# Gated recurrence of the second block: one half of the tokens reversed, both halves in one matmul per level

## The chip, the cores and the metric

The kernel runs on one core of a Trainium2 chip. Its time is the device time of one execution, in microseconds; of several runs the median is taken. Before the change it is 829.94 us (three runs, 829.58 to 829.96).

## What is computed

The reference is a chain of blocks on 256 tokens of width 1024, all in fp32: a block with a linear recurrence and a feed-forward part, a block with stick-breaking attention and a feed-forward part, and then a "second block" with two branches side by side, a block attention (moba) and a gated linear recurrence (hgrn). The change is in the last of these. Cut to what matters:

```python
kb = (1.0 - lb) * jax.nn.sigmoid(-fpre)            # 4 heads, 128 key dims
qb = jax.nn.silu(bq)                               # queries
vb = bi                                            # values
# per chunk of 64 tokens, g = log_f, the logarithm of the forget gate
cum = jnp.cumsum(gc, axis=2)
o_inter = jnp.einsum('bhtk,bhkv->bhtv', qc * jnp.exp(cum), state)
diff = jnp.where(causal[:, :, None], cum[:, :, :, None, :] - cum[:, :, None, :, :], LOG_DECAY_MASK)
scores = jnp.einsum('bhtk,bhsk,bhtsk->bhts', qc, kc, jnp.exp(diff))
o_intra = jnp.einsum('bhts,bhsv->bhtv', scores, vc)
last = cum[:, :, -1:, :]
state = state * jnp.exp(last[:, :, 0, :, None]) + jnp.einsum('bhsk,bhsv->bhkv', kc * jnp.exp(last - cum), vc)
```

So the score of query t and key s is a sum over 128 dimensions of q times k times the product of the forget gates between s and t.

## The kernel before, in words

**Matmuls.** Every large product is done as three fp32r matmuls: weights and activations are split into a high part and a remainder (wh and wl, xh and xl), and high x high, low x high and high x low are added in PSUM. Weights come in 266 pieces of 512 KB, loaded by SP's queue some pieces ahead (`load_ahead`). ACT or DVE rounds them to wh (`round`), and DVE subtracts to get wl (`tt` at L239). All matmuls but the transposes are recorded by the helper `mm` at L281 to L283, so they share one line of the profile and are told apart by their tiles.

**Order.** The program is written by a planner (`Run`). The matmul stream is the main thread. Work of other engines stands in small tasks (`spawn`) that yield the planner's time at which they may go on; between two products the planner polls them (`poll`, L343) and then rounds weights ahead (`prep_ahead`, L461). Its clocks for PE, DVE and ACT come from costs that are written in the code. What it leaves is a fixed queue for each engine, and each queue runs in order.

**The second block.** `proj4` (L1278) projects four groups of 128 columns into PSUM and `evac` (L1270) multiplies with the row of norm factors on DVE: queries `qb`, forget gates `fb`, and further on `aq`, `ag`, `bg`, `ak` for the attention and the output gates. `proj_t` (L1295) does the same with tokens on the partitions, for values (`vbt`); its evacuation on ACT scales with a column. `ORDER_E` (L50) sets the order of these groups after queries and gates: aq, g0, bi, ag, bg, ak, g1, g2, g3, av, ple. In the matmul stream they alternate with the recurrence, which is spread among them by the planner.

**The recurrence** works by levels instead of chunks. `diag` (L1359) multiplies keys and queries of each of the four heads and each half of 128 tokens (eight 128 x 128 products) and keeps the diagonal in `dg`. Then, for a level of block size b = 1, 2, 4, ... 64 and at last 128, a key of an earlier block meets a query of the later block next to it. `levels` (L1415) keeps keys K (tile ga_) and queries Q (tile hq) in place: after each level it multiplies the keys of earlier blocks and the queries of later blocks by the gate products of a block (tiles gf_ and ht). `level_scores` (L1376) does a level's matmuls: for b under 32 (LONE) one for each head and each half, all 128 keys against the 64 queries in later blocks:

```python
for g in range(8 if b < LONE else 0):
    a, i = divmod(g, 2)
    rhs = Q[:, a, 128 * i:128 * i + 128].rearrange("p (n two b) -> p n two b", two=2, b=b)[:, :, 1, :]
    r.mm(bank.t[:, 64 * g:64 * g + 64], K[:, a, 128 * i:128 * i + 128], rhs, bank.start(), True)
```

A masked copy on DVE (L1408) then puts the blocks that belong together into `dg`. For b of 32 and 64 each pair of blocks has its own matmul, and ACT copies the result. Level 128 takes the keys of the first half to the queries of the second, and ACT copies it to `xg`. `hgrn_out` (L1580) multiplies values with `dg` and `xg`, twelve matmuls. An fp32 matmul (not fp32r) shows in the trace as two records. In between stand the small groups of the attention's head norms: `hsq` with a constant (sums of squares), and `rtx` with `sel` (roots spread over the rows).

Of the kernel before, what the change touches and what calls it, by code (L numbers as in the profile page):

```python
# [107 lines left out]
LEVELS = [1, 2, 4, 8, 16, 32, 64]  # L108

# [7 lines left out]
def make_consts():  # L117
# [13 lines left out]
    m = np.zeros((128, 7 * 64), np.int32)  # L131
    for n, b in enumerate(LEVELS):
        t = np.array([t for t in range(128) if t % (2 * b) >= b])
        m[:, n * 64:(n + 1) * 64] = (p[:, None] // (2 * b) == t[None, :] // (2 * b)) & (p[:, None] % (2 * b) < b)
# [53 lines left out]
class Run:  # L188
# [324 lines left out]
    def gemm_t(self, banks, name, k, ms, x, stop):  # L513

        self.need(x, f"{name} {k}")
        wh, wl = self.weight(name, k, ms)
        for t, b in enumerate(banks):
            s = slice(128 * t, 128 * t + 128)
            self.mm(b.t, x.hi[:, s], wh, b.start(), False)
            self.mm(b.t, x.lo[:, s], wh, False, False)  # L520
            self.mm(b.t, x.hi[:, s], wl, False, stop)
            self.tick()
# [33 lines left out]
def build(r):  # L556
# [9 lines left out]
    msk = r.one("msk", [128, 448], I32)  # L566
# [703 lines left out]
    def evac(bank, dst, done=None, more=None):  # L1270
        yield r.pe_t + 0.2
        yield norm.s
        t = r.tt(dst, v2(bank), bc2(norm.S), OP.mult)
        r.free(bank, t)
        if done is not None:
            done.t = t

    def proj4(base, dst, done, outer=False, tag="acc"):  # L1278

        if outer:  # L1280
# [4 lines left out]
            for p in range(2):  # L1285
                r.spawn(evac(bs[p], dst[:, 2 * p:2 * p + 2], done[p]))
        else:
            for p in range(2):
# [4 lines left out]
                r.spawn(evac(b, dst[:, 2 * p:2 * p + 2], done[p]))  # L1293

    def proj_t(base, vs):  # L1295
# [4 lines left out]
        for k in range(8):  # L1300
            r.gemm_t(bs, "w_in2", k, quad(base), norm.x[k], k == 7)

        def chain(t):
            yield r.pe_t + 0.2
            yield norm.s
            f = r.act(vs[t].v, bs[t].t, AF.Copy, scale=norm.col[:, t:t + 1])
# [6 lines left out]
    qb, fb = r.big("qb"), r.big("fb")  # L1313
    q_done, f_done, aq_done, ak_done, ag_done, bg_done = ([Fut(), Fut()] for _ in range(6))
    vbt, va = [Fut(), Fut()], [Fut(), Fut()]
    proj4(16, qb, q_done, True, "g")
# [17 lines left out]
    proj4(20, fb, f_done)  # L1334

    def forget():
        yield f_done

        A, N, F = r.big("ga_"), r.big("gn_"), r.big("gf_")
# [5 lines left out]
        for c in range(4):  # L1345
            t = r.ts(A[:, c], A[:, c], oml[:, c:c + 1], None, OP.mult)
# [3 lines left out]
        for c in range(4):  # L1350
            r.ts(N[:, c], N[:, c], lbv[:, c:c + 1], 1.0, OP.mult, OP.add)
# [4 lines left out]
    dg, xg = r.big("dg", [128, 8, 128]), r.big("xg", [128, 4, 128])  # L1356
    dgf, lvl = Fut(), [Fut() for _ in range(8)]

    def diag():  # L1359
        yield [qf, kf, Avail("g", 2)]  # L1360
        for i in range(2):
            b = r.bank("g")
            for g in range(4):
                c = slice(128 * (g % 2), 128 * (g % 2) + 128)
                a = 2 * i + g // 2
                r.mm(b.t[:, 128 * g:128 * g + 128], hg["K"][:, a, c], qb[:, a, c], b.start(), True)
            yield r.pe_t + 0.2
            t = r.tt(dg[:, 4 * i:4 * i + 4], b.t.rearrange("p (a b) -> p a b", b=128),
# [4 lines left out]
    def halves(ap, b):  # L1373
        return ap.rearrange("p h (n two b) -> p (h n) two b", two=2, b=b)

    def level_scores(n, b, K, Q):  # L1376
        yield Avail("g", 1)
        bank = r.bank("g")
        if b == 128:
            for a in range(4):  # L1380
                r.mm(bank.t[:, 128 * a:128 * a + 128], K[:, a, 0:128], Q[:, a, 128:256], bank.start(), True)
# [5 lines left out]
        for g in range(8 if b >= LONE else 0):  # L1387
            a, i = divmod(g, 2)
            for j in range(64 // b):
                o = 128 * i + 2 * b * j  # L1390
                r.mm(bank.t[2 * b * j:2 * b * j + b, 64 * g + b * j:64 * g + b * j + b], K[:, a, o:o + b],
                     Q[:, a, o + b:o + 2 * b], g == 0, True)
        for g in range(8 if b < LONE else 0):
            a, i = divmod(g, 2)
            rhs = Q[:, a, 128 * i:128 * i + 128].rearrange("p (n two b) -> p n two b", two=2, b=b)[:, :, 1, :]
# [414 lines left out]
```

## Time and profile before

| | |
|---|---|
| median of three runs | 829.94 us |
| profiled execution, its own time | 829.69 us |
| its span, from the first to the last instruction | 828.0 us |
| granted TensorE clock, mean | 0.999 |
| TensorE matmuls busy | 821.9 us (99%) |
| weight loads busy (beside matmuls) | 734.5 us (89%) |
| VectorE busy | 627.6 us (76%) |
| ScalarE busy | 388.1 us (47%) |
| GpSimd busy | 23.9 us (3%) |
| chain of work that ended last: TensorE's share | 96% |

The span is cut into windows where single stretches are read; the recurrence lies between 617 and 662 us of it, among the projections of the second block. A row of the time line names start, length, engine, line, operation and tiles; a matmul's length includes the depth of its pipeline, so the cost of a group is read from its start to the start of the next.

### The profile page before, as it was taken

To read this page: it belongs to the slowest core of one execution; us is meant where nothing else is said; L and a number is where in the kernel's file an instruction comes from. 1 tells how busy PE (TensorE), PEld (TensorE's weight loads), DVE (VectorE), ACT (ScalarE), POOL (GpSimd) and SP (SyncE) were. 2 spreads that over 40 slices of the span, in tenths; PEclk is the share of its full clock that TensorE was granted. 3 is DMA by queue.
4 is the path that set the end of the run, shared out by engine and by line. 5 is a ranking of instruction groups with operands and counts; after the bars stand their busy time and mean duration, and the time that the engine had idled before them with its cause. 6 is when DMAs were issued, how large, how long until landed. Compare 5 with 4: busy or idle time off the path is not lost.

```text
span 828.0 us, 13459 instructions
## 1 busy us (share of the span) xinstructions
PE 821.9 (99%) x5206; PEld 734.5 (89%) x5206; DVE 627.6 (76%) x1213; ACT 388.1 (47%) x735; POOL 23.9 (3%) x56
## 2 busy tenths in 40 slices
PE   9999999999999999999999999999999999999997
PEld 8999988888888898999888888888999999999997
DVE  5999998685764668898899667546788886896872
ACT  4788475241222545565566123115353354686421
POOL 1300000000000001011000000001000000000000
PEclk9999999999999999999999999999999999999999
DMA  8945666654644223355776464543433434456401
GB/s 323 393 145 206 237 221 220 213 206 164 216 149 157 77 102 141 140 179 178 233 251 227 168 215 159 197 152 130 138 123 108 178 129 138 171 201 202 155 2 51
DMA packets 41360, 144.79 MB, mean 175 GB/s; under 512 B 4616, under 2 KB 5904, under 8 KB 41296
## 3 DMA queue, kind: packets, MB, share of 16 engines
q1 hardware_dynamic: 40896, 142.61, 49.1%
q0 software_dynamic: 400, 1.32, 0.5%
q8 instruction: 41, 0.67, 0.3%
q14 instruction: 23, 0.19, 0.1%
HBM read 142.85 MB, written 1.06 MB: 174 GB/s over the span
## 4 chain that ended last, share of the span: by engine, by line
PE 96%; DVE 2%; DMA 1%; ACT 1%; SPq 1%; issue 0%
PE acc L283 51%; PE g L283 42%; PE g L1044 1%; DMA raw<-in_weights 1%; PE g L1199 1%; DVE rec L243 1%; DVE wl L239 0%; PE g L1100 0%; ACT wh L264 0%; PE g L1540 0%; SPq L406 0%; SPq L399 0%; DVE z L239 0%; ACT sq L266 0%; DVE o L239 0%
## 5 line engine op out<-in xcount | busy, mean ns | idle before, releaser
L239 DVE TENSOR_TENSOR wl<-raw,wh 128x512 fp32r<-128x512 f32 x518 | 336.4, 690 | 20.2 <-ACT wh L264 11.5
L264 ACT ACTIVATE wh<-raw 128x512 fp32r<-128x512 f32 x357 | 196.7, 624 | 35.3 <-PE acc L283 18.1
L283 PE MATMUL g<-wh,xh 128*128 128x512 f32 x368 | 144.6, 393 | 0.0
L283 PE MATMUL g<-wl,xh 128*128 128x512 f32 x368 | 143.4, 390 | 0.0
L283 PE MATMUL g<-wh,xl 128*128 128x512 f32 x368 | 143.2, 389 | 0.0
L283 PE MATMUL acc<-xh,wh 128*128 128x256 f32 x416 | 120.5, 290 | 0.0
L283 PE MATMUL acc<-xl,wh 128*128 128x256 f32 x416 | 117.6, 283 | 0.0
L283 PE MATMUL acc<-xh,wl 128*128 128x256 f32 x416 | 117.6, 283 | 0.0
L283 PE MATMUL acc<-wh,hx 128*128 128x512 f32 x352 | 108.8, 390 | 0.0
L283 PEld LDWEIGHTS acc<-xh,wh 128*128 128x128 f32 x416 | 79.5, 191 | 4.4 <-issue 3.9
L283 PEld LDWEIGHTS g<-wl,xh 128*128 128x128 f32 x368 | 69.1, 188 | 14.6
L283 PEld LDWEIGHTS g<-wh,xl 128*128 128x128 f32 x368 | 69.2, 188 | 13.8
L283 PEld LDWEIGHTS g<-wh,xh 128*128 128x128 f32 x368 | 69.1, 188 | 13.8
L283 PEld LDWEIGHTS acc<-xl,wh 128*128 128x128 f32 x416 | 79.7, 192 | 0.1
L264 ACT ACTIVATE hx<-g 128x512 fp32r<-128x512 f32 x22 | 12.1, 596 | 144.4 <-PE g L1044 144.4
L283 PEld LDWEIGHTS acc<-xh,wl 128*128 128x128 f32 x416 | 79.6, 191 | 0.0
L283 PEld LDWEIGHTS acc<-wh,hx 128*128 128x128 f32 x352 | 65.8, 188 | 13.4
L283 PE MATMUL acc<-wl,hx 128*128 128x512 f32 x176 | 68.5, 389 | 0.0
L254 DVE CAST wh<-raw 128x512 fp32r<-128x512 f32 x161 | 68.4, 425 | 0.0
L243 DVE SCALAR_TENSOR_TENSOR gu<-g,ny,gu 128x512 f32<-128x512 f32 (+1 forms) x24 | 16.2, 706 | 54.3 <-PE g L283 54.2
L283 PE MATMUL g<-xh,wh 128*128 128x256 f32 x136 | 39.5, 290 | 0.0
L283 PEld LDWEIGHTS acc<-wl,hx 128*128 128x128 f32 x176 | 33.0, 188 | 6.9
(294 smaller groups left out, 1370.4 us busy)
## 6 DMA issues: line engine op xcount, KB each, us to landing
raw<-in_weights SPq DMA_DIRECT2D x264, 512.0 KB, 3.7
toep<-vrev POOLq DMA_DIRECT2D x2, 512.0 KB, 4.8
raw<-in_weights SPq DMA_DIRECT2D x3, 256.0 KB, 5.0
gh<-in_x SPq DMA_DIRECT2D x3, 256.0 KB, 5.4
past<-in_past SPq DMA_DIRECT2D x1, 384.0 KB, 4.1
raw<-in_weights SPq DMA_DIRECT2D x2, 128.0 KB, 2.4
pt<-in_p POOLq DMA_DIRECT2D x1, 256.0 KB, 5.4
out_y<-o__1285_8421 SPq DMA_DIRECT2D x1, 256.0 KB, 2.4
```

The lines of the kernel that those rows point to most:

```text
L239: self.nc.vector.tensor_tensor(out, a, b, op)
L243: self.nc.vector.scalar_tensor_tensor(out, a, s, b, op0=op0, op1=op1)
L254: self.nc.vector.tensor_copy(out, a)
L264: self.nc.scalar.activation(out, a, f, scale=scale, **kw)
L283: self.nc.tensor.matmul(out, l, r, start=start, stop=stop, skip_group_check=True)
L1044: nc.tensor.transpose(b.t[:, at:at + 128], w[:, t, 256 * p + 128 * i:256 * p + 128 * i + 128], r.ident)
L1199: nc.tensor.transpose(tb[a].t[:, b], m[:, a, b], r.ident)
```

## The change

The second half of the tokens is kept in reverse order throughout the recurrence, and tiles are laid out by half first (`by_half`: 128 partitions, half, head, 128 tokens). In the reversed half the earlier blocks of a level stand where the later ones stand in the first half. So the keys of both halves' earlier blocks together fill 128 columns, and one matmul takes them against the later blocks of both halves. Of its 128 x 128 results the masked copies keep the two parts that belong together. In detail:

- `evac` with `turn` writes `qb` and `fb` in two instructions, the second half reversed. `forget`, `diag` and the products of the levels work on the new layout, with as many instructions as before.
- `stand`: for b = 1, 2, 4, 8, 16 and 64 ACT copies the keys of the earlier blocks of both halves into one operand (tile hm). Then four matmuls, one for each head, replace eight. Level 32 keeps its sixteen small ones, level 128 its four.
- The masked copy on DVE, and the copies on ACT for b of 32 and 64, are done once for each half; the mask grows from 448 to 640 columns (five levels of 128).
- Values must be reversed in their tokens too. `turn_x` copies the second half of the norm's output in reverse (tiles xrh, xrl, four ACT copies), `gemm_t` takes these as the operand of the second token half of `bi`, and `turn_col` reverses the scale row on ACT (tile nr), turns it into a column by a matmul of one column with a constant, and copies it (tile nc).
- `hgrn_out` reads `xg` and the second half of `dg` backwards.

```diff
-    def gemm_t(self, banks, name, k, ms, x, stop):
+    def gemm_t(self, banks, name, k, ms, x, stop, turned=None):
...
+            hi, lo = x.hi[:, s], x.lo[:, s]
+            if turned is not None and t == 1:
+                self.need(turned, "turned")
+                hi, lo = turned.hi, turned.lo
...
-    def evac(bank, dst, done=None, more=None):
+    def evac(bank, dst, done=None, turn=False):
...
+        if turn:
+            r.tt(dst[:, 0], v2(bank)[:, :, 0:128], bc2(norm.S)[:, :, 0:128], OP.mult)
+            t = r.tt(dst[:, 1], v2(bank)[:, :, 128:256][:, :, ::-1], bc2(norm.S)[:, :, 128:256][:, :, ::-1],
+                     OP.mult)
+        else:
+            t = r.tt(dst, v2(bank), bc2(norm.S), OP.mult)
...
+    def turn_col():
+
+        yield norm.s
+        yield Avail("g", 1)
+        row = r.small("nr", 128)
+        yield r.act(row[0:1], norm.S[0:1, 128:256][:, ::-1], AF.Copy) + 0.06
+        b = r.bank("g")
+        r.mm(b.t[:, 0:1], row[0:1], ones128[0:1, 0:1], True, True)
+        yield r.pe_t + 0.2
+        colr.v = r.small("nc", 1)
+        t = r.act(colr.v, b.t[:, 0:1], AF.Copy)
...
+    def turn_x():
+
+        hi, lo = r.big("xrh", [128, 8, 128], F32R), r.big("xrl", [128, 8, 128], F32R)
+        for q in range(2):
+            yield [norm.x[4 * q + i] for i in range(4)]
+            yield r.pe_t + 3.0
+            c = slice(4 * q, 4 * q + 4)
+            for d, s in ((hi, norm.hi[q]), (lo, norm.lo[q])):
+                t = r.act(d[:, c], s[:, :, 128:256][:, :, ::-1].bitcast(F32), AF.Copy)
+                yield t
...
+    def blocks(ap, b, at, step):
+
+
+        (ps, pn), (hs, _), (_, a), (_, n) = ap.ap
+        return bass.AP(tensor=ap.tensor, offset=ap.offset + at, ap=[[ps, pn], [hs + step, 2], [2 * b, a * n // (2 * b)],
+                                                                    [1, b]])
...
+    def stand(n, b, K):
+
+        M[n].v = r.big("hm", [128, 4, 128])
+        src = earlier(K, b).rearrange("p i n b -> p n i b")
+        M[n].t = r.act(M[n].v.rearrange("p a (n i b) -> p (a n) i b", i=2, b=b), src, AF.Copy)
+
     def level_scores(n, b, K, Q):
+        if b < 128 and b != LONE:
+            stand(n, b, K)
+            yield M[n].t + 0.06
...
-        for g in range(8 if b < LONE else 0):
-            a, i = divmod(g, 2)
-            rhs = Q[:, a, 128 * i:128 * i + 128].rearrange("p (n two b) -> p n two b", two=2, b=b)[:, :, 1, :]
-            r.mm(bank.t[:, 64 * g:64 * g + 64], K[:, a, 128 * i:128 * i + 128], rhs, bank.start(), True)
+        nb = 64 // b
+        to = bank.t.rearrange("p (i a t) -> p i a t", i=2, a=4)
...
+        else:
+            for a in range(4):
+                r.mm(to[:, :, a], M[n].v[:, a], later(Q[:, :, a:a + 1], b), bank.start(), True)
...
-            nc.vector.copy_predicated(out, m, src)
-            t = r._v((512 + 66) / 0.96)
+            for i in range(2):
+                m = msk[:, 128 * n + 64 * i:128 * n + 64 * i + 64].rearrange("p (n b) -> p n b", b=b)
+                out = dg[:, i].rearrange("p a (n two b) -> p a n two b", two=2, b=b)[:, :, :, 1 - i]
+                nc.vector.copy_predicated(out, m[:, None].to_broadcast([128, 4, nb, b]),
+                                          to[:, i].rearrange("p a (n b) -> p a n b", b=b))
...
-            k, q = halves(K, b)[:, :, 0, :], halves(Q, b)[:, :, 1, :]
-            r.tt(k, k, Tv[:, :, 1:2].to_broadcast([128, nb, b]), OP.mult)
-            t = r.tt(q, q, Tv[:, :, 0:1].to_broadcast([128, nb, b]), OP.mult)
+            k, q = earlier(K, b), later(Q, b)
+            r.tt(k, k, decays(U, b, 1, -1), OP.mult)
+            t = r.tt(q, q, decays(U, b, 0, 1), OP.mult)
...
-            r.mm(o[:, 128:256], vbt[0].v[:, v], xg[:, a], False, False)
-            r.mm(o[:, 128:256], vbt[1].v[:, v], dg[:, 2 * a + 1], False, True)
+            r.mm(o[:, 128:256], vbt[0].v[:, v], xg[:, a, ::-1], False, False)
+            r.mm(o[:, 128:256], vbt[1].v[:, v], dg[:, 1, a, ::-1], False, True)
...
-            proj_t(24, vbt)
+            proj_t(24, vbt, True)
```

The planner orders the queues anew. The scale's matmul (cst with ny, four) stands six matmuls earlier in PE's queue than before; 21 matmuls of the stream further on stands the new one of one column. Counted from a common point of the stream (70 steps ahead of the scale's matmul before, 64 after), 223 steps of the stream stand ahead of level 1 before and 202 after. The queues are shown at two places. The first is PE at the level with b = 4, which is the third, in the middle of the values' projection (`bi`). There rtx with sel is the first spread of roots, the rows with ga_ or hm are the level, and xrh and xrl are the turned x. Before:

```order
L283 MATMUL acc_6281<-wh_6219,xh_5428 128x512
L283 MATMUL acc_6281<-wh_6219,xl_5430 128x512
L283 MATMUL acc_6281<-wl_6220,xh_5428 128x512
L283 MATMUL g_6299<-hq_6129,ga__952_6001 128x64 x8
L283 MATMUL g_6308<-rtx_6260,sel_5917 128x256 x4
L283 MATMUL acc_6282<-wh_6219,xh_5428 128x512
L283 MATMUL acc_6282<-wh_6219,xl_5430 128x512
```

After:

```order
L288 MATMUL acc_6294<-wh_6273,xh_5428 128x512
L288 MATMUL acc_6294<-wh_6273,xl_5430 128x512
L288 MATMUL acc_6294<-wl_6274,xh_5428 128x512
L288 MATMUL g_6325<-rtx_6292,sel_5928 128x256 x4
L288 MATMUL g_6330<-hq_6118,hm_6313 128x2x64 x4
L288 MATMUL acc_6295<-wh_6273,xrh_5622 128x512
L288 MATMUL acc_6295<-wh_6273,xrl_5623 128x512
```

The spread now stands ahead of the level instead of behind it, the level has four matmuls instead of eight, and six more wide steps of `bi` stand ahead of both.

The second place is ACT from the sums of squares (hsq) to the roots rtx, through the first three levels. Before, no level has a row on ACT here:

```order
L266 ACTIVATE hsq_6152<-aq_5922 128x1024
L264 ACTIVATE wh_6157<-raw_5957 128x512
L277 ACT_TABLE_LOAD
L266 ACTIVATE rt_6180<-g_6170,der 128x256 x2
L266 ACTIVATE rt_6180<-rt_6180 128x256 x2
L264 ACTIVATE wh_6219<-raw_6013 128x512 x2
L264 ACTIVATE rtx_6260<-y_6179 128x256
```

After:

```order
L269 ACTIVATE hm_6168<-ga__955_5998 128x512
L271 ACTIVATE hsq_6178<-aq_5933 128x1024
L269 ACTIVATE wh_6180<-raw_5990 128x512
L282 ACT_TABLE_LOAD
L271 ACTIVATE rt_6217<-g_6203,der 128x256 x2
L271 ACTIVATE rt_6217<-rt_6217 128x256 x2
L269 ACTIVATE hm_6232<-ga__955_5998 128x512
L269 ACTIVATE wh_6234<-raw_6030 128x512
L269 ACTIVATE wh_6273<-raw_6068 128x512
L269 ACTIVATE rtx_6292<-y_6216 128x256
L269 ACTIVATE wh_6273<-raw_6068 128x512
L269 ACTIVATE hm_6313<-ga__955_5998 128x512
```

Three copies of key blocks stand between the rest. On DVE, between the evacuation of `qb` and rtx, there are one rounding and one 128 x 512 instruction more than before; up to hq there are two 128 x 512 instructions less.

## Rows read from the trace of the kernel before

**Rows 1.** The page, busy time of each engine: us, share of the span, instructions.

```profile
PE 821.9 (99%) x5206; PEld 734.5 (89%) x5206; DVE 627.6 (76%) x1213; ACT 388.1 (47%) x735; POOL 23.9 (3%) x56
```

**Rows 2.** Waits of PE in the whole run: us in total, times, longest us.

```profile
PE g L588 <- DVE der L607: 1.1, 1, 1.1
PE acc L283 <- DVE rec L243: 0.4, 1, 0.4
```

**Rows 3.** Windows over the recurrence: us, then busy us (instructions) of PE, PEld, DVE, ACT, POOL; clock, DMA.

```profile
600.00:620.00 20.00, 20.00 (x171) 20.00 (x171) 17.64 (x38) 10.04 (x12) 0.00 (x0) 1.00 0.32 110
620.00:640.00 20.00, 20.00 (x156) 18.67 (x155) 17.91 (x31) 8.88 (x17) 0.00 (x0) 1.00 0.36 129
640.00:660.00 20.00, 20.00 (x177) 18.30 (x176) 17.65 (x33) 5.79 (x11) 0.00 (x0) 1.00 0.49 175
```

**Rows 4.** Time line, PE at levels 1, 64 and 128: start us, length us, instruction, records.

```profile
625.31 1.90 PE L283 MATMUL g<-hq,ga__952_6001 128*128 128x64 f32 x16
627.01 0.36 PE L283 MATMUL acc<-xh,wh 128*128 128x256 f32 x1
...
653.54 1.15 PE L283 MATMUL g<-hq,ga__952_6001 128*64 128x64 f32 x16
654.62 0.39 PE L283 MATMUL acc<-xh,wh 128*128 128x256 f32 x1
...
656.88 1.06 PE L283 MATMUL g<-hq,ga__952_6001 128*128 128x128 f32 x8
657.69 0.36 PE L283 MATMUL acc<-xh,wh 128*128 128x256 f32 x1
```

**Rows 5.** Time line, PE at the norm's sums, four matmuls of one column.

```profile
591.38 0.28 PE L283 MATMUL acc<-xh,wl 128*128 128x256 f32 x1
591.50 0.95 PE L283 MATMUL g<-ones,ssq 128*128 128x1 f32 x8
592.31 0.36 PE L283 MATMUL acc<-xh,wh 128*128 128x256 f32 x1
```

**Rows 6.** Time line, ACT at the last norm and at level 128; in brackets idle before.

```profile
582.64 0.91 ACT L264 ACTIVATE xh<-gh,der 128x256 fp32r<-128x256 f32 x2 [4.12 <-DVE gh L239]
...
657.97 0.60 ACT L264 ACTIVATE xg<-g 128x512 f32<-128x512 f32 x1 [2.13 <-PE g L283]
```

**Rows 7.** Time line, DVE from the evacuation of qb to rtx.

```profile
605.26 1.29 DVE L239 TENSOR_TENSOR qb<-g,S 128x512 f32<-128x512 f32 x2 [2.12 <-ACT S L264]
...
607.66 0.42 DVE L254 CAST wh<-raw 128x512 fp32r<-128x512 f32 x1
608.11 0.69 DVE L239 TENSOR_TENSOR wl<-raw,wh 128x512 fp32r<-128x512 f32 x1
608.72 0.69 DVE L248 TENSOR_SCALAR gn__953_6002<-fb 128x1024 f32<-128x1024 f32 x1
...
621.02 1.22 DVE L239 TENSOR_TENSOR hq<-qb,gf__954_6003 128x1024 f32<-128x1024 f32 x1
...
627.24 0.69 DVE L239 TENSOR_TENSOR ga__952_6001<-ga__952_6001,gf__954_6003 128x512 f32<-128x512 f32 x1 [1.53 <-PE g L283]
...
628.46 0.42 DVE L239 TENSOR_TENSOR ht<-ht 128x256 f32<-128x256 f32 x1
628.79 0.42 DVE L239 TENSOR_TENSOR rt<-rt 128x256 f32<-128x256 f32 x1
...
635.05 0.46 DVE L239 TENSOR_TENSOR rtx<-y,rtx 128x256 fp32r<-128x256 f32 x1
```

**Rows 8.** Instructions on tile dg, the masked copies: duration ns min/median/max, first and last start.

```profile
L1408 DVE COPY_PREDICATED dg<-msk,g x5: 708/720/1322, 629.6 to 648.5; 128x512 f32<-128x512 int32 x5
```

**Rows 9.** Time line, PE in the values' projection and at the first spread.

```profile
633.42 0.40 PE L283 MATMUL acc<-wh,xl 128*128 128x512 f32 x1
633.66 0.39 PE L283 MATMUL acc<-wl,xh 128*128 128x512 f32 x1
...
636.96 0.72 PE L283 MATMUL g<-rtx,sel 128*128 128x256 f32 x4
```

More of the change, by code (lines that the diff above doesn't have):

```diff
@@ L1276, in evac, with proj4 @@
             done.t = t
-    def proj4(base, dst, done, outer=False, tag="acc"):
+    def proj4(base, dst, done, outer=False, tag="acc", turn=False):
         if outer:
@@ L1285, in proj4 @@
             for p in range(2):
-                r.spawn(evac(bs[p], dst[:, 2 * p:2 * p + 2], done[p]))
+                r.spawn(evac(bs[p], two(dst, p, turn), done[p], turn))
         else:
@@ L1292, in proj4, with proj_t @@
                         r.gemm(b, c, "w_in2", k, base + 2 * p + c, norm.x[k], k == 7)
-                r.spawn(evac(b, dst[:, 2 * p:2 * p + 2], done[p]))
-    def proj_t(base, vs):
+                r.spawn(evac(b, two(dst, p, turn), done[p], turn))
+    def proj_t(base, vs, turn=False):
         bs = [r.bank("acc"), r.bank("acc")]
@@ L1300, in proj_t @@
         for k in range(8):
-            r.gemm_t(bs, "w_in2", k, quad(base), norm.x[k], k == 7)
+            r.gemm_t(bs, "w_in2", k, quad(base), norm.x[k], k == 7, turned[k] if turn else None)
         def chain(t):
@@ L1305, in chain @@
             yield norm.s
-            f = r.act(vs[t].v, bs[t].t, AF.Copy, scale=norm.col[:, t:t + 1])
+            col = norm.col[:, t:t + 1]
+            if turn and t == 1:
+                yield colr
+                col = colr.v
+            f = r.act(vs[t].v, bs[t].t, AF.Copy, scale=col)
             r.free(bs[t], f)
@@ L1311, in proj_t, with two @@
             r.spawn(chain(t))
-    qb, fb = r.big("qb"), r.big("fb")
+    def turn_col():
[8 more added lines that the diff above has]
+        t = r.act(colr.v, b.t[:, 0:1], AF.Copy)
+        r.free(b, t)
+        colr.t = t
+    def turn_x():
[7 more added lines that the diff above has]
+                yield t
+            for k in range(4 * q, 4 * q + 4):
+                turned[k].hi, turned[k].lo, turned[k].t = hi[:, k], lo[:, k], t
+    def two(dst, p, turn):
+        return dst[:, :, 2 * p:2 * p + 2] if turn else dst[:, 2 * p:2 * p + 2]
+    colr, turned = Fut(), [Fut() for _ in range(8)]
+    r.spawn(turn_x())
+    r.spawn(turn_col())
+    by_half = [128, 2, 4, 128]
+    qb, fb = r.big("qb", by_half), r.big("fb", by_half)
     q_done, f_done, aq_done, ak_done, ag_done, bg_done = ([Fut(), Fut()] for _ in range(6))
     vbt, va = [Fut(), Fut()], [Fut(), Fut()]
-    proj4(16, qb, q_done, True, "g")
+    proj4(16, qb, q_done, True, "g", True)
     def x2_chain():
@@ L1410, in level_scores @@
         r.free(bank, t)
         lvl[n].t = t
+    M = [Fut() for _ in range(8)]
     read = [Fut() for _ in range(8)]
```

90 lines of the change are left out of this document (48 added, 42 removed).

## The prediction

> **What bounds the kernel now.** I read the page's busy times first, then TensorE's waits, then the time line of the recurrence. TensorE (PE) is busy 99% of the span, VectorE (DVE) comes next with 76% [rows 1]. A modelled busy share proves little by itself, so the list of waits counts more: in the whole run PE waits for another engine twice, 1.1 us at the start and 0.4 us once later [rows 2]. The three windows over the recurrence say the same: PE 20.00 us of 20.00, granted clock 1.00 (the 2.4 GHz level) [rows 3]. So a microsecond taken out of PE's queue here comes out of the time, as long as no other engine comes late. DVE could: it is busy 17.64, 17.91 and 17.65 us in the three windows [rows 3], 53.2 of 60, which leaves 6.8 us. ScalarE (ACT) has 24.7 of 60 and is not short of time.
>
> **The levels on PE.** I name a level by its block size b. Before, a level with b from 1 to 16 is eight matmuls with 128 weight columns and 64 moving columns: 16 records, from 625.31 to the next group at 627.01, 1.70 us, 106 ns a record [rows 4]; the other four levels have the same row. After, such a level is four matmuls with 128 weight columns and 128 moving columns. That shape is in the trace: level 128 has four of them, 8 records, from 656.88 to 657.69, 0.81 us, 101 ns a record [rows 4]. So the number of records sets the time, and twice the moving columns cost nothing. Five levels save 5 x (1.70 - 0.81) = **4.45 us**. Level 64 goes from eight matmuls with 64 weight columns, 653.54 to 654.62, 1.08 us [rows 4], to four of the new kind, 0.81: **0.27 us**. Level 32 keeps its sixteen 32 x 32 matmuls, and the diagonal, level 128 and the output keep their counts: nothing.
>
> Two things that PE does after aren't in the rows. The new matmuls write two runs of 64 columns that lie 256 columns apart; the old ones wrote one run. And the output's moving operand is read backwards in eight matmuls of two records. Bounds: nothing, or twice the time of the records concerned, 6 x 0.81 = 4.9 us for the first and 16 x 0.10 = 1.6 us for the second. A gain is excluded, since neither has fewer records. I take nothing for both: level 1 reads every second value and pays 106 ns a record where the contiguous level 128 pays 101 [rows 4], and a write of 64 values in a run is far from that. The Trainium skill has a rule against the first: "PSUM — Partial Sum Buffer", section "Specifications (TRN2)", says of PSUM's 8-byte lines that any non-contiguous access pattern slows matmuls significantly. No row here shows such a write; by this rule nearly nothing of the gain would be left (rival B, priced there from rows).
>
> **What is added on PE.** One matmul turns the scale row into a column: 128 weight columns, one moving column, two records. Four matmuls of one column take 8 records and 0.81 us, 591.50 to 592.31 [rows 5], so two records are 0.20; and the first matmul behind such a group takes 0.36 us [rows 4] where one in the stream takes 0.28 [rows 5], 0.08 more: **+0.28 us**. The spread of the roots (rtx, sel) stood behind a level twice and now once, which is one more change between the two kinds: **+0.08 us**. PE in sum: -4.45 - 0.27 + 0.28 + 0.08 = **-4.36 us**.
>
> **What is added elsewhere, and its cover.** ACT gets six copies of the key blocks (hm), four that turn x, the turned row and its column; a 128 x 512 copy takes 0.60 us [rows 6], so this is some 6.5 us on an engine with 35 us free. The first two copies of x stand ahead of ACT's next xh, where it idled 4.12 us [rows 6]: nothing. The second two stand behind the last xh and delay two roundings; DVE has 2.12 us to spare behind these before the scale arrives at 605.26 [rows 7]: nothing, and 1.2 us if that cover were gone. The mask's transfer grows by 98 KB long before the first masked copy: nothing.
>
> DVE: evacuating in halves makes eight instructions of 0.33 us (628.46 to 628.79 [rows 7]) out of four of 0.61 (608.11 to 608.72): +0.2 us. The five masked copies of 128 x 512 took 0.71 to 1.32 us, median 0.72 [rows 8]; they become ten of 128 x 256. A half may cost half as much or as much as the whole. I take a little over half, since a 128 x 256 product takes 0.33 where a 128 x 512 one takes 0.61: +0.2 us over the five. The in-place products keep their count and size: nothing.
>
> **Who comes late.** A level's chain is now product on DVE, copy on ACT, matmul. PE's queue is in order, so what counts is where each group stands in it.
>
> Level 1: PE has 21 fewer steps of 0.12 us (591.38 to 591.50 [rows 5]) ahead of it and the turned column's matmul more: 625.31 - 2.51 + 0.28 = 623.1, and the hsq group now stands behind it, so a little earlier still. It needs hq, which DVE began at 621.02 and had in 1.22 us [rows 7]. The scale's matmul stands six steps earlier (-0.72), the halves cost 0.2, and two 128 x 512 instructions fewer stand ahead (-1.2): hq ends at 620.5. Margin 2 us.
>
> The tightest place is the first spread, rtx with sel. Before, PE reached it at 636.96 [rows 9], and DVE's rtx ended at 635.05 + 0.46 = 635.51 [rows 7]. After, PE is there at 636.96 - 2 x 0.89 (levels 1 and 2) - 1.70 (level 4 now stands behind it) + 0.28 + 6 x 0.24 (six wide steps more ahead; 633.42 to 633.66 [rows 9]) = 635.2. DVE: 635.51 - 0.72 + 0.2 + 0.45 (one rounding more; 607.66 to 608.11 [rows 7]) + 0.6 (one 128 x 512 more) = 636.0 if it idles as before. But 1.53 us of that was the wait for level 1's matmuls ahead of the first in-place product, at 627.24 [rows 7]; these now end before 624, and DVE's queue gets to the product at about 624.7. So 634.5. A wait of nothing to 0.8 us; I take **0.1**. The later levels' products stand 1 to 2 us ahead of their matmuls, and ACT's copy needs 0.6 of that.
>
> Over the stretch DVE's 6.8 free microseconds shrink by 4.3 (PE is shorter) and 0.9 (halves, rounding): 1.6 left. Behind the recurrence the counts on every engine are as before, so nothing there gives the gain back.
>
> **Sum.** -4.36 + 0.1 = -4.26 us against the profiled run's 829.69: 825.4. The median of the three runs, 829.94, lies 0.25 above that run, so I forecast **825.7**.
>
> **The rivals.**
> A. *DVE comes late*, because half a masked copy costs what the whole did. Then up to 1.3 us each come on top for the two levels ahead of rtx, and 0.7 each for the next three: 4.7 us against 1.6 free. PE waits 3.1 us, first at rtx: 828.8, between 827.3 and 829.5. For it: these copies are already the only DVE instructions of one shape that cost up to 1.8 times their median [rows 8]. Against: products halve with their columns.
> B. *Four matmuls cost what eight did*, because a two-run write takes twice as long or goes out as two. Then 6 x 0.81 = 4.9 us come back: 830.6. This is also the case in which the change doesn't do what it says. For it: no row shows such a write. Against: the runs are 64 values long, and records are set by weight columns [rows 4]. It is what the Trainium skill's rule on the page named above would give.
> C. *Slower: DVE becomes the bound of the levels.* The 14 in-place products run over both halves with a new outer step. At 1.83 times their 0.61 us (the ratio 1.32 to 0.72 [rows 8]) each costs 0.5 more, 7 us in all, and with A's 4.7 DVE is 11.7 - 1.6 = 10.1 us short: 835.8. It decides from 7.6 us of added DVE work on (1.6 free, 4.3 of gain, 1.7 for the bound below). Against: level 1's product already works on single values, at 0.69 us (627.24 [rows 7]).
>
> **How the numbers follow.** 0.2% (1.7 us, so 828.28) is about what a measurement of this kernel can tell from no change. Forecast, 825.0 to 826.8: 0.74. A: 0.13, of which 0.06 lies below 828.28. B: 0.08, no change. C: 0.05, slower. Faster 0.80, same 0.15, slower 0.05. The range goes down to 825.0 (no wait, both added terms of PE at nothing, and 0.2 for the spread of the three runs), and up to 828.2, into A.
>
> **What would show it.** Right: the groups of hq and hm have 8 records and 0.81 us to the next group; PE is busy about 4.3 us less; no wait of PE over 0.5 us in the recurrence; hm copies at 0.60 us. A would show halves of over 0.7 us and PE waiting for DVE at rtx; B 8 records over 1.6 us, or 16; C in-place products over 1 us. What would make it wrong otherwise is a wait in the attention that follows, where DVE and ACT share the softmax.

## The result and the profile after

The changed kernel takes 824.88 us (median of four runs, 824.49 to 824.99); runs of the kernel before beside it gave 829.76 (829.52 to 829.96). The ratio is 0.9944, with a 95% interval of 0.9933 to 0.9956: faster by 4.9 us, and the interval says 3.7 to 5.6. The forecast was 825.7. The range went down to 825.0; the median lies 0.1 below that, and the ratio times the 829.94 of before gives 825.3, inside. The profiled run took 824.98 with a span of 823.3, against 829.69 and 828.0: 4.7 us less on both.

The page's busy times, which answer to [rows 1]:

```profile
span 823.3 us, 13385 instructions
PE 817.4 (99%) x5160; PEld 730.3 (89%) x5160; DVE 630.1 (77%) x1228; ACT 391.6 (48%) x744; POOL 23.9 (3%) x56
```

PE is still busy 99%, and has 4.5 us and 46 records less: six levels with 8 records less each, and two records more for the turned column. Waits of PE in the whole run, to [rows 2]:

```profile
PE g L598 <- DVE der L617: 1.1, 1, 1.1
PE g L288 <- DMA raw<-in_weights: 0.3, 1, 0.3
```

The first is the start's wait, as before. The short ones behind it come and go from run to run in the first 40 us. There is none in the recurrence. The windows over the recurrence, to [rows 3], same columns (PE, PEld, DVE, ACT, POOL, clock, DMA):

```profile
600.00:620.00 20.00, 20.00 (x168) 19.85 (x168) 19.16 (x45) 11.95 (x17) 0.00 (x0) 1.00 0.32 107
620.00:640.00 20.00, 20.00 (x147) 18.34 (x146) 19.90 (x38) 10.87 (x19) 0.00 (x0) 1.00 0.42 134
640.00:660.00 20.00, 20.00 (x180) 19.00 (x179) 19.21 (x39) 7.57 (x16) 0.00 (x0) 1.00 0.72 233
```

PE fills its windows at the same clock as before. DVE has gone from 53.2 of 60 us to 58.3; between 620 and 640 it idles 0.1 us. Now the levels on PE, to [rows 4] (start, length, instruction, records): level 1, the first spread of roots with level 4 behind it, level 32, level 64.

```profile
622.42 1.07 PE L288 MATMUL g<-hq,hm 128*128 128x128 f32 x8
623.24 0.36 PE L288 MATMUL acc<-xh,wh 128*128 128x256 f32 x1
...
635.24 0.64 PE L288 MATMUL g<-rtx,sel 128*128 128x256 f32 x4
635.71 1.06 PE L288 MATMUL g<-hq,hm 128*128 128x128 f32 x8
636.52 0.47 PE L288 MATMUL acc<-wh,xrh 128*128 128x512 f32 x1
...
649.72 0.46 PE L288 MATMUL g<-hq,ga__955_5998 128*32 128x32 f32 x32
650.11 0.39 PE L288 MATMUL acc<-xh,wh 128*128 128x256 f32 x1
...
654.16 1.05 PE L288 MATMUL g<-hq,hm 128*128 128x128 f32 x8
654.98 0.36 PE L288 MATMUL acc<-xh,wh 128*128 128x256 f32 x1
```

A level of the new kind takes 0.81 or 0.82 us from its start to the next group, where it took 1.70. The turned column's matmul, with the steps of the stream around it:

```profile
606.00 0.28 PE L288 MATMUL acc<-xh,wl 128*128 128x256 f32 x1
606.21 0.38 PE L288 MATMUL g<-ones,nr 1*128 1x1 f32 x2
606.51 0.39 PE L288 MATMUL acc<-xh,wh 128*128 128x256 f32 x1
606.74 0.28 PE L288 MATMUL acc<-xl,wh 128*128 128x256 f32 x1
```

It takes 0.30 us itself, and the steps ahead of it and behind it take 0.21 and 0.23 where a step of the stream takes 0.12. Level 32 had the same 32 records before, and took longer:

```profile
649.89 0.70 PE L283 MATMUL g<-hq,ga__952_6001 128*32 128x32 f32 x32
650.51 0.50 PE L283 MATMUL acc<-wh,xh 128*128 128x512 f32 x1
```

0.62 us before, 0.39 after. DVE around the first spread, to [rows 7] and [rows 9], and its masked copies, to [rows 8] (number, then ns at least, median, at most):

```profile
626.12 1.33 DVE L1488 COPY_PREDICATED dg<-msk,g 128x256 f32<-128x256 int32 x2
627.23 0.73 DVE L244 TENSOR_TENSOR gate<-acc,S 128x512 f32<-128x512 f32 x1
...
632.95 1.32 DVE L1488 COPY_PREDICATED dg<-msk,g 128x256 f32<-128x256 int32 x2
634.05 0.46 DVE L244 TENSOR_TENSOR rtx<-y,rtx 128x256 fp32r<-128x256 f32 x1
```

```profile
L1488 DVE COPY_PREDICATED dg<-msk,g x10: 431/442/802, 626.1 to 648.3; 128x256 f32<-128x256 int32 x10
```

Two halves of a masked copy take 1.11 us from start to next at the levels 1 and 2, the same as the whole did, and about 0.66 at the others. DVE ends rtx at 634.05 + 0.46 = 634.51, and PE takes it at 635.24, 0.73 us later. On ACT the copies of key blocks (hm), to [rows 6]:

```profile
L269 ACT ACTIVATE hm<-ga__955_5998 128x512 f32<-128x512 f32 x6 | 4.1, 676 | 7.3 <-DVE ga__955_5998 L244 7.3
```

### The profile page after: what moved, and what is told of

It reads as the page before. It is cut to its first block, busy times and chain, and to the rows that moved or that the text cites. A ratio compares the mean times of both kernels' runs of the same rounds, so it can differ in the third digit from the quotient of the medians.

```text
span 823.3 us, 13385 instructions
## 1 busy us (share of the span) xinstructions
PE 817.4 (99%) x5160; PEld 730.3 (89%) x5160; DVE 630.1 (77%) x1228; ACT 391.6 (48%) x744; POOL 23.9 (3%) x56
## 4 chain that ended last, share of the span: by engine, by line
PE 98%; DVE 1%; DMA 0%; ACT 0%; issue 0%; SPq 0%
PE acc L288 51%; PE g L288 44%; PE g L1054 1%; PE g L1209 1%; DVE rec L248 1%; PE g L1110 0%; PE g L1622 0%; DMA raw<-in_weights 0%; DVE z L244 0%; ACT rt L271 0%; DVE o L244 0%; DVE wl L244 0%; DVE rt L244 0%; ACT o L271 0%; SPq L404 0%
## 5 line engine op out<-in xcount | busy, mean ns | idle before, releaser
L269 ACT ACTIVATE wh<-raw 128x512 fp32r<-128x512 f32 x350 | 193.6, 624 | 35.2 <-PE acc L288 18.1
L259 DVE CAST wh<-raw 128x512 fp32r<-128x512 f32 x168 | 71.4, 425 | 0.0
```

Source lines behind the costliest of these rows:

```text
L259: self.nc.vector.tensor_copy(out, a)
L269: self.nc.scalar.activation(out, a, f, scale=scale, **kw)
```

## The experiments

Each kernel below ran with runs of the kernel before beside it on the same chip; these gave medians of 829.4 to 829.5 us. The changed kernel has three medians on record, that of the result among them: 824.54 to 825.03. What was expected stands as it was written ahead of the run.

**1. Eight matmuls again, nothing else.** The key operand, the turned tokens, the copies and every engine's order stay as in the changed kernel. Only the query blocks of the two halves move apart.

```diff
-                r.mm(to[:, :, a], M[n].v[:, a], later(Q[:, :, a:a + 1], b), bank.start(), True)
+                for i in range(2):
+                    r.mm(to[:, i, a], M[n].v[:, a], later(Q[:, :, a:a + 1], b)[:, i], bank.start(), True, i > 0)
```

> The changed kernel with one part undone: the key blocks of both halves still stand in one operand, but the query blocks of the two halves move in two matmuls of 64 columns instead of one of 128, at all six levels that have this operand. Nothing else changes its place on any engine. Theory 1 (a record costs what its 128 weight columns cost, whatever moves): each level has 16 records again and takes 1.70 us instead of 0.82, six levels give back 6 x 0.88 = 5.3 us, and the time is 824.9 + 5.3 = 830.2, that of the kernel before. Theory 2 (a record costs by its moving columns): 16 records of half the length, 0.82 us a level, 824.9. Theory 3 (the gain comes from elsewhere, the masked copies or the order): the levels take 1.70 us, but the time is well under 830.

Measured: 830.07 us (829.68 to 830.61), ratio 1.0008, 0.9999 to 1.0018. Time line of PE at level 1:

```profile
622.18 1.90 PE L288 MATMUL g<-hq,hm 128*128 128x64 f32 x16
623.89 0.36 PE L288 MATMUL acc<-xh,wh 128*128 128x256 f32 x1
```

Half the moving columns in twice the matmuls: 1.71 us, and 1.70 or 1.71 at the other five levels. A record of 128 weight columns costs 0.10 to 0.11 us whether 64 columns move or 128, and the whole gain of the change hangs on that: with it undone, and everything else kept, the time is within 0.2% of that of the kernel before. That is theory 1: the median lies 5.0 to 5.5 us above the three medians of the changed kernel, for 5.3.

**2. Does the way a level is written matter?** The same four matmuls, but the results go to single values four columns apart.

```diff
-                r.mm(to[:, :, a], M[n].v[:, a], later(Q[:, :, a:a + 1], b), bank.start(), True)
+                r.mm(bank.t[:, a::4], M[n].v[:, a], later(Q[:, :, a:a + 1], b), bank.start(), True)
```

> The changed kernel, with the four matmuls of a level at all six levels writing their 128 results as single values four columns apart, instead of in two runs of 64 (the four matmuls interleave and fill the bank; the scores land in the wrong columns, so the output is not the reference's). Same instructions, same places. In the changed kernel a level takes 0.82 us (622.42 to 623.24) against 0.81 for level 128, which writes one run of 128. Theory 1 (the weights' columns set a record's time, and the write is hidden behind it whatever its pattern): 0.82 us a level, 824.9. Theory 2 (it is only the length of the runs that hid it, and single values write at half the pace): up to 1.6 us a level, 6 x 0.8 = 4.9 us, 829.8. The Trainium skill (PSUM - Partial Sum Buffer, Specifications (TRN2)) speaks for theory 2: any non-contiguous pattern slows matmuls significantly.

Measured: 824.79 us (824.47 to 825.01), ratio 0.9941, 0.9926 to 0.9957. PE at level 1:

```profile
621.92 1.07 PE L288 MATMUL g<-hq,hm 128*128 128x128 f32 x8
622.75 0.36 PE L288 MATMUL acc<-xh,wh 128*128 128x256 f32 x1
```

0.83 us, and 0.81 to 0.82 at the other five. Writing single values costs nothing here, so two runs of 64 could not cost anything either. The Trainium skill's rule ("PSUM — Partial Sum Buffer", "Specifications (TRN2)") that any non-contiguous pattern slows matmuls significantly doesn't hold for these fp32 matmuls of 128 moving columns; the measurement decides.

**3. Rival A's price, set on purpose.** Each masked copy is made twice.

```diff
                 nc.vector.copy_predicated(out, m[:, None].to_broadcast([128, 4, nb, b]),
                                           to[:, i].rearrange("p a (n b) -> p a n b", b=b))
+                nc.vector.copy_predicated(out, m[:, None].to_broadcast([128, 4, nb, b]),
+                                          to[:, i].rearrange("p a (n b) -> p a n b", b=b))
```

> The changed kernel with each of the ten masked copies made twice (the same values again, the output is the reference's). This is rival A's price set on purpose: VectorE gets 2 x 1.11 us for the levels 1 and 2 (626.12 to 627.23 for a pair) and 3 x 0.66 for the other three, 4.2 us in all. Theory 1 (VectorE has nothing left but the idle time that the windows show, 0.84 + 0.10 + 0.79 us between 600 and 660): TensorE waits 4.2 - 1.7 = 2.5 us, time 827.4. Theory 2 (only the first spread of roots is tight): rtx ended at 634.51 and TensorE was there at 635.24, so 2.2 us more ahead of it make a wait of 1.5 us there, and what comes later has its own margin: 826.4. Theory 3 (margins everywhere): no wait, 824.9.

Measured: 829.32 us (829.08 to 829.59), ratio 0.9998, 0.9989 to 1.0008. All of the gain is gone, more than any of the theories had. Time line of DVE at level 1:

```profile
626.47 0.73 DVE L1488 COPY_PREDICATED dg<-msk,g 128x256 f32<-128x256 int32 x1
627.24 0.74 DVE L1490 COPY_PREDICATED dg<-msk,g 128x256 f32<-128x256 int32 x1
627.78 0.79 DVE L1488 COPY_PREDICATED dg<-msk,g 128x256 f32<-128x256 int32 x1
628.61 0.75 DVE L1490 COPY_PREDICATED dg<-msk,g 128x256 f32<-128x256 int32 x1
629.15 0.72 DVE L244 TENSOR_TENSOR gate<-acc,S 128x512 f32<-128x512 f32 x1
```

Waits of PE from 600 us on:

```profile
PE g L288 <- DVE rtx L244: 1.6, 1, 1.6
PE g L288 <- DVE hq L244: 1.2, 2, 0.8
PE acc L288 <- DVE wl L244: 0.3, 1, 0.3
```

My price of the second copy was wrong: it writes where the first one just wrote and starts only when that has ended (627.24 after 626.47 + 0.73). Four copies take 2.68 us at level 1 where two took 1.11, and 1.61 at level 4 (642.26 to 643.87) where two took 0.67; over the five levels some 6.0 us are added, not 4.2. Most of it comes out as time: the median rose by 4.4 us, PE's queue from the second half's diagonal to the output is 4.2 us longer (616.84 to 667.09, against 616.49 to 662.50), and the first wait is at rtx, as rival A said. Theory 1's sum with the right price, 6.0 - 1.7 of idle time = 4.3, comes out, but not for its reason. Of the 1.7 us that the windows show idle, 0.8 lie between 600 and 620, ahead of the first masked copy, and this run leaves them idle too: its three windows still hold 1.5 us. What took up most of the rest is DVE's idle time behind the first masked copy, up to the evacuation of ag: 3.3 us in the changed kernel (626.12 to 663.13), 2.4 of it just ahead of ag, and 2.1 us here (626.47 to 667.73).

**4. Level 32.** The same 32 records, written to two groups of 32 rows, as before, instead of four.

```diff
-                        r.mm(to[o:o + b, i, a, b * j:b * j + b], K[:, i, a, o:o + b], Q[:, i, a, q:q + b], a == 0, True)
+                        w = 2 * b * j
+                        r.mm(to[w:w + b, i, a, b * j:b * j + b], K[:, i, a, o:o + b], Q[:, i, a, q:q + b], a == 0 and i == 0, True)
...
```

ACT's copy at this level reads and writes the same rows as the matmuls.

> The changed kernel with one thing at level 32: its sixteen matmuls of 32 x 32 write rows 0 to 31 and 64 to 95 for both halves (two groups of 32 weight columns of the array, as in the kernel before), where the changed kernel writes the second half's at rows 32 and 96 (all four groups). The order of every engine is the same; the second half's scores of this level land in the wrong rows, so the output is not the reference's. Level 32 took 0.62 us before and 0.39 after, a gain that the prediction had as nothing. Theory 1 (groups that differ work side by side, so that four finish sooner than two): 0.62 us again, the rest as in the changed kernel. Theory 2 (its neighbours in the queue set it): 0.39 us.

```profile
649.64 0.70 PE L288 MATMUL g<-hq,ga__955_5998 128*32 128x32 f32 x32
650.27 0.39 PE L288 MATMUL acc<-xh,wh 128*128 128x256 f32 x1
```

0.63 us against 0.39: theory 1. (This kernel ran once and is read for this row alone; its 825.16 us tells nothing of 0.2 us.) In the second half, reversed, the earlier block of a pair stands where the first half has its later one, so its keys fall to the other two groups of rows, and matmuls in different groups run side by side. The Trainium skill says so ("TensorEngine Tiling (Array Packing)", "Tiling Modes"): tiles work independently, and 32 columns make four of them. The trace agrees, with 0.63 to 0.39.

**5. The kernel before, without reversal, in small matmuls.** If records of 32 weight columns are that cheap, is the joint operand needed at all? The levels 1 to 16 of the kernel before, a block of 32 keys with the 16 queries of its own 32 tokens; the results stand in 128 columns, and four masked copies of 32 x 128 a level replace one of 128 x 512.

```diff
-            rhs = Q[:, a, 128 * i:128 * i + 128].rearrange("p (n two b) -> p n two b", two=2, b=b)[:, :, 1, :]
-            r.mm(bank.t[:, 64 * g:64 * g + 64], K[:, a, 128 * i:128 * i + 128], rhs, bank.start(), True)
+            for j in range(4):
+                o = 128 * i + 32 * j
+                rhs = Q[:, a, o:o + 32].rearrange("p (n two b) -> p n two b", two=2, b=b)[:, :, 1, :]
+                r.mm(sm[32 * j:32 * j + 32, g], K[:, a, o:o + 32], rhs, g == 0, True, j > 0)
...
```

> The kernel before, without any reversal, with the levels 1 to 16 in 32 matmuls of 32 weight and 16 moving columns instead of eight of 128 and 64, and the masked copies in four of 32 x 128. It asks whether the gain needs the two halves in one operand at all. Level 32 has 32 records of 32 weight columns in both kernels, but in the kernel before they stand in two of the four groups of 32 columns of the array and take 0.62 us (649.89 to 650.51), in the changed one in all four and take 0.39. Theory 1 (the four groups work side by side): 64 records take 2 x 0.39 = 0.78 us a level instead of 1.70, 5 x 0.92 = 4.6 us less, 825.3, without a copy or a turned operand. Theory 2 (0.62 us is what 32 such records cost in the company of this kernel): 1.24 us a level, 2.3 us less, 827.6. Theory 3 (a record has a floor that 64 of them feel): no gain, 829.9 or more.

Measured: 825.41 us (825.21 to 826.10), ratio 0.9954, 0.9939 to 0.9969.

```profile
625.93 0.74 PE L283 MATMUL g<-hq,ga__952_6001 128*32 128x16 f32 x64
626.60 0.39 PE L283 MATMUL acc<-xh,wh 128*128 128x256 f32 x1
```

64 records in 0.67 us, less than the 0.82 of the joint operand. The levels give 5 x 1.03 = 5.2 us, of which 4.1 reach the time. Some 0.5 of the difference lies in the steps around these groups (0.21 us ahead and 0.22 behind, where it was 0.12 and 0.21), and in the last window PE stands idle for 0.15 us. This kernel needs no turned operand, no copies of keys and no turned column, and its interval overlaps that of the change. The gain belongs to what a record costs, and the joint operand is one way to take it.

**6. Both, and who is next.** The changed kernel with its levels 1 to 16 in sixteen matmuls of 32 x 32, and forty masked copies of 32 x 64.

```diff
+                for j in range(4 if b < LONE else 0):
+                    p = slice(32 * j, 32 * j + 32)
+                    ...
+                    r.mm(sm[p, :, a], M[n].v[:, a, p], rhs, a == 0, True, j > 0)
...
```

> The changed kernel, with the levels 1 to 16 in sixteen matmuls of 32 weight and 32 moving columns instead of four of 128 and 128: a block of 32 keys of the joint operand meets only the queries of the same 32 tokens. Level 32 has this shape in the changed kernel, 32 records in 0.39 us (649.72 to 650.11), against 0.82 us for a level of four. The result stands in 128 columns, and the masked copies become forty of 32 x 64 instead of ten of 128 x 256. Theory 1 (TensorE still sets the time): 5 x (0.82 - 0.39) = 2.1 us less, 822.8. Theory 2 (VectorE has become the bound of this stretch, 19.90 us busy of 20 from 620 to 640): TensorE waits for what it saves, 824.9, or later if eight short copies cost more than the two (0.66 or 1.11 us).

Measured: 824.42 us (823.92 to 824.67), ratio 0.9940, 0.9925 to 0.9955. PE at level 1, then DVE at its masked copies, then the last two windows:

```profile
621.93 0.28 PE L288 MATMUL acc<-xh,wl 128*128 128x256 f32 x1
622.13 0.46 PE L288 MATMUL g<-hq,hm 128*32 128x32 f32 x32
622.53 0.39 PE L288 MATMUL acc<-xh,wh 128*128 128x256 f32 x1
622.75 0.28 PE L288 MATMUL acc<-xl,wh 128*128 128x256 f32 x1
```

```profile
625.29 1.81 DVE L1499 COPY_PREDICATED dg<-msk,g 32x64 f32<-32x64 int32 x8
627.13 0.69 DVE L244 TENSOR_TENSOR wl<-raw,wh 128x512 fp32r<-128x512 f32 x1
```

```profile
620.00:640.00 20.00, 20.00 (x220) 17.35 (x219) 19.61 (x51) 11.24 (x20) 0.00 (x0) 1.00 0.43 150
640.00:660.00 20.00, 19.37 (x230) 17.77 (x229) 19.56 (x49) 9.23 (x20) 0.00 (x0) 1.00 0.65 213
```

From its start to the next a level takes the 0.4 us that theory 1 wanted. But the step ahead of it takes 0.20 us (621.93 to 622.13) where the changed kernel has 0.12, and the one behind 0.22 instead of 0.20, so PE's queue gains about 0.3 a level, 1.6 in all and not 2.1. The time falls by 0.1 to 0.6 (824.42 against the three medians of the changed kernel), so most of the 1.6 doesn't reach it: theory 2. The eight copies take 1.84 us where the two took 1.11, PE now waits in the last window, and DVE is full. Two steps followed. First I took work from DVE: fewer copies at levels 1 and 16, and rounding leaned to ACT within the recurrence (`r.LEAN = 1.5` there instead of -0.15).

> The changed kernel with the 32 x 32 matmuls of e7_small at the levels 1 to 16, and two edits that take work from VectorE in this stretch: the masked copies of the levels 1 and 16 in four of 32 x 128 instead of eight of 32 x 64 (a copy of 32 x 64 took 0.19 us from start to next in e7_small, whatever its 64 values), and the planner's rounding of weights leans to ScalarE while the recurrence runs. In e7_small the levels took 0.40 us each on TensorE, 2.1 us less in all, but the time fell by 0.3 to 0.5 only, and VectorE was busy 19.61 and 19.56 us of 20. Theory 1 (VectorE took the rest): up to 2 x 4 x 0.19 = 1.5 us come from the copies and 0.45 for each rounding moved; TensorE's 2.1 us come through nearly whole: 822.9 to 823.4. Theory 2 (something else took it, such as the change between kinds of matmuls or the wait for weights from memory): 824.4 as e7_small.

Measured: 824.04 us (823.91 to 824.61), ratio 0.9934, 0.9918 to 0.9950. A miss: with rounding leaned, DVE still had nine roundings between 600 and 662, against ten, and four copies of 32 x 128 at level 1 took 1.82 us, what the eight had. DVE stayed at 19.7 and 19.6 us of 20. Then the diagonal went into 32 x 32 matmuls too:

> e8_small_lean, and the diagonal in 32 x 32 matmuls too: 32 of them, 64 records, instead of eight of 128 and 128, 16 records, 1.62 us. Its product with the unit matrix becomes four of 32 x 256 instead of two of 128 x 512 (same columns on VectorE), and GpSimd, idle there, clears the score tile. b1_small shows 64 such records in 0.67 us (625.93 to 626.60). Theory 1 (TensorE sets the time): 0.95 us under e8_small_lean, 821.9 to 822.5. Theory 2 (VectorE is the bound from here on): the same as e8_small_lean.

Measured: 824.54 us (824.28 to 825.04), ratio 0.9939, 0.9924 to 0.9955; the changed kernel beside it, on the same chip:

> The changed kernel again, on the same chip as the three runs beside it: 824.9, ratio 0.994 to the kernel before.

Measured: 824.54 us (824.18 to 825.27), ratio 0.9937. The diagonal fell from 1.62 to 0.69 us on PE, the levels from 4.1 to 1.9; with the steps around them that is some 2.5 us of PE's queue, and nothing of it reached the time. PE's waits of e10_best name the cause:

```profile
PE acc L288 <- DVE wl L244: 1.5, 2, 0.8
```

These are waits for weights that DVE rounds. Ahead of the recurrence, from 580 to 600, DVE has 5.6 us free in e10_best, and ACT idles for 14.83 us up to 603.36. So the last kernel, otherwise e10_best, prepares weights there, 24 tiles ahead instead of 12:

```diff
+    r.MIN_AHEAD = 24
     proj4(16, qb, q_done, True, "g", True)
...
     proj4(20, fb, f_done, turn=True)
+    r.MIN_AHEAD = Run.MIN_AHEAD
```

> e10_best, and the planner prepares the weights 24 tiles ahead instead of 12 while the queries and the forget gates are projected, when VectorE is busy 7.0 and 6.8 of 10 us (580 to 600) and ScalarE stands idle from 588 to 603. In e10_best the levels and the diagonal took 3.0 us less on TensorE than in the changed kernel and the time did not fall (824.54 against 824.54): TensorE waited for rounded weights, 1.5 us at two places, and VectorE was busy 19.6 of 20 us. Theory 1 (VectorE's sum in this stretch is the bound): rounding moved out of it comes back as time, each 128 x 512 being 0.45 and 0.61 us of VectorE; 822.0 to 823.6. Theory 2 (the order of the chain, not the sum of the work, is the bound): 824.5.

Measured: 823.39 us (823.01 to 824.13), ratio 0.9929, 0.9913 to 0.9946. Since its gain over the changed kernel was of the size of the intervals, both ran once more side by side:

> The changed kernel, for comparison with f2_ahead on one chip: 824.5 to 825.0.

> e12_ahead again, beside the changed kernel on one chip and in more rounds. Theory 1 (VectorE's work in this stretch was the bound, and moving roundings ahead of it gave 1.1 us): 1.0 to 1.5 us under f1_after, ranges of single runs apart or nearly so. Theory 2 (the difference between the two earlier calls was the chips'): within 0.5 us of f1_after.

Measured: 825.03 us (824.62 to 825.16), ratio 0.9947, 0.9935 to 0.9960, and 823.18 us (822.64 to 823.34), ratio 0.9925, 0.9911 to 0.9938. The single runs of the two don't meet: 1.85 us. Windows of f2_ahead:

```profile
600.00:620.00 20.00, 20.00 (x224) 19.68 (x224) 17.77 (x45) 10.93 (x15) 0.00 (x0) 1.00 0.32 113
620.00:640.00 20.00, 20.00 (x189) 17.34 (x189) 18.73 (x40) 12.52 (x23) 0.00 (x0) 1.00 0.41 133
```

PE is full again in these two (19.68 of 20 in the third), and DVE has 2.2 and 1.3 us free where the changed kernel left it 0.8 and 0.1. This version beats both kernels, and the sum fits the PE savings that gave nothing while DVE was full: 2.5 us less in PE's queue, against 0.6 us of waiting that is left ahead of the level with b = 8 (645.86 to 646.78, where the two steps take 0.33 without it), is 1.9, and 1.85 was measured. Preparing weights ahead without the small matmuls was not tried; the changed kernel has no wait in the recurrence that it could remove.

## Why the prediction was right, and where it was off

**What bounds the kernel.** Right, and experiment 1 shows it: 5.3 us put back on PE alone came back as 5.0 to 5.5 us of time. The gain is a gain on PE.

**The levels.** Right to the hundredth of a level: five levels from 8.50 to 4.07 us, 4.43 for 4.45, and 1.08 - 0.82 = 0.26 for 0.27 at level 64. The row that carried it was level 128 in the trace of before. Experiment 1 shows that the moving columns, 64 or 128, don't set a record's time; that the weight columns do is in [rows 4], 67 ns a record for 64 weight and 64 moving columns where 128 weight and 64 moving take 106. At level 64 the ends count too: the step ahead of it took 0.21 us before (653.33 to 653.54) and takes 0.12 now, the one behind 0.22 and now 0.20, so the level gave 0.37.

**The two unknown costs on PE.** I took nothing for the write in two runs and nothing for the output's reversed reads. Both right: 0.81 to 0.82 us a level against 0.81 for level 128, no more with single values (experiment 2), and the output's group takes 2.60 us in both kernels (658.84 to 661.44 before, 659.90 to 662.50 after). The argument for the first was an inference from the reading side; experiment 2 is the evidence.

**Added on PE.** The turned column was mis-sized: 0.50 us for 0.28. Its matmul takes 0.30 for 0.20, the step behind it 0.11 more for 0.08, and the step ahead of it 0.09 more, which I had at nothing. The spread of the roots was given 0.08 for a change of kind more, and cost nothing. Its two groups took 0.55 and 0.57 us before, each right behind a level (636.96 to 637.51), and take 0.47 and 0.48 now, behind the stream; but the steps behind the levels with b = 4 and 8 now take 0.08 or 0.09 more than in the stream: nothing in sum.

**Level 32 was mis-sized.** "Level 32 keeps its sixteen 32 x 32 matmuls: nothing" was true of the number and false of the time. It fell by 0.23 us, for the cause that experiment 4 shows. The row that could have told was in the trace of before: 0.62 us for 32 records in two groups of rows. I counted records and didn't look where they stand.

**Added elsewhere.** The halves of the evacuations take 0.34 us each (four from 604.43 to 605.77) for 0.33. The copies of key blocks on ACT take 0.68 us in the mean for 0.60: 0.86 at level 1 and 0.68 at level 2, where runs are one and two values long, 0.62 and 0.63 otherwise. ACT had the time, and no wait of PE names it.

**DVE and the tightest place.** PE was forecast at the first spread at 635.2 and came at 635.24; rtx was forecast to end at 634.5 and ended at 634.51. That PE's figure is so close is partly luck: the turned column cost 0.2 more, but the start was 0.1 earlier and the six wide steps took 0.23 us each and not 0.24. Between these two numbers lay a margin of 0.7 us, and I still took a wait of 0.1 out of caution; there was none. The idle time left to DVE was forecast at 1.6 us of 60 and is 1.7 by the windows. But half of it, 0.8, lies between 600 and 620, ahead of the levels' products and copies; behind the first masked copy 0.9 us is left up to 660. How tight this is, experiment 3 shows: 6.0 us more on DVE gave 4.4 us of time.

**The rivals.** A's condition did not come about: a half took 0.44 us (median), where the whole took 0.72, and 1.11 for both at levels 1 and 2. Its mechanism is real, with the place that it named, and DVE's slack was the right number to fear. B did not come: a level has 8 records and takes 0.81 or 0.82 us, and experiment 2 writes single values at the same price. C did not come: the in-place products take 0.69 us at every level.

**The sum.** Forecast -4.26 us, measured -4.71 from profiled run to profiled run. The rows above give -4.43 (five levels) - 0.37 (level 64) + 0.50 (turned column) + 0.00 (spreads) - 0.25 (level 32, with the steps at its ends) = -4.55. The last 0.16 is mostly the start: at 578 us the same step stands 0.1 earlier, which differs as much between any two runs. So the forecast missed 0.25 at level 32 and 0.1 each at level 64, the spreads and the wait, all towards a larger gain, and 0.22 the other way at the turned column. That is 0.3 of the 0.8 us between the forecast and the median. Of the rest, 0.2 is that the kernel before gave 829.76 beside it where the forecast started from 829.94, and the start and the spread of runs make up what is left. The lower end of the range had only added terms set to nothing; it allowed for no operation that becomes faster.

## What to carry to other kernels

Count matmuls of fp32 by their records and price a record by its weight columns: as long as 128 moving columns cost what 64 do, moving more per matmul is free, and 32 weight columns spread over all four groups of rows are cheaper still. When a kernel is bound by one engine, write down the idle time of the next one in the same stretch before taking anything away: here a change of 4.7 us left 1.7 us of it, half of that ahead of the place where it was needed, and the next 2.5 us taken from PE's queue were worth nothing until rounding was moved out of the stretch. A group's price includes the steps of the stream ahead of it and behind it. An instruction count that stays the same is no reason to take the time as unchanged when the change moves where the operands stand.

## What the runs showed of the hardware that I had not expected

- 32 records of 32 weight columns take 0.38 to 0.40 us when they are spread over four groups of rows and 0.62 to 0.63 when they stand in two; 64, spread over four, take 0.66 to 0.69.
- Steps of the stream of 128 x 256 take 0.12 us. The last one ahead of a group of 32 or 64 weight columns, or of the turned column's matmul, takes 0.20 to 0.21, and the first one behind takes 0.22 to 0.23. Around the groups of 128 x 128 the step ahead stays at 0.12, and the one behind takes 0.20 to 0.21.
- An fp32 matmul that writes single values 16 bytes apart takes as long as one that writes a run (0.81 to 0.83 us for eight records).
- A masked copy of 128 x 256 takes 0.42 to 0.45 us when its runs have four values or more, and 0.72 to 0.80 with one or two. One of 32 x 64 takes 0.19 to 0.24 us from start to next, so eight of them cost more than the two of 128 x 256 that they replace. One that writes where the last one wrote starts only at its end (627.24 behind 626.47 + 0.73 in experiment 3); one that writes elsewhere starts earlier (627.78, within 627.24 + 0.74).
